# Products with the weights' low parts moved to the end of each step, and the activations' sums begun during the output projection, at an offset of 224 bytes

## The chip, the cores and the metric

The kernel runs on one core of a Trainium2 chip. The metric is device time of one execution in microseconds (us); lower is better. Before the change the median of three runs is 2220.28 us (2219.53 to 2221.06).

The engines are named as in the profile: PE is TensorE, which multiplies (PEld is its loading of the stationary operand); DVE is VectorE; ACT is ScalarE; POOL is GpSimd; SP issues most of the transfers from memory.

## The reference: what is computed

Two layers of a transformer-like trunk on one sequence of 256 tokens, width 2048, in float32:

```python
for l in range(2):
    h = rmsnorm(x, ...)
    x = x + (even_mixer(h, ...) if l == 0 else dilated_attention(h, w_qkv, w_o))
    h = rmsnorm(x, f_norm[l])
    x = x + (silu(h @ w1) * (h @ w3)) @ w2      # 2048 -> 5632 -> 2048
return rmsnorm(x, final_norm)
```

The first layer's mixer has an input projection, an mLSTM and a gated linear recurrence side by side, and an output projection; the second layer's is attention with 16 heads between two projections. Nearly all of the work is products of 256 rows of activations with weights that are read once, about 400 MB in all.

## The kernel before

**Numbers in two parts.** TensorE multiplies float32 at full pace only in a reduced form (fp32r). So each operand is split: a high part, rounded to that form, and a low part, the rest. ScalarE casts the weights to `wh` (line 228) and VectorE subtracts to get `wl` (line 229); activations are stored as pairs in the same way (`xT`, `hT`, `oT`, `ya`, `yb`; index 0 is the high part, 1 the low part). A product is then three products: high by high, high by low, low by high.

**Items and steps.** The weights come in items of 512 contraction rows by 512 columns (1 MB, one transfer into `raw`, three buffers). Each item is two steps, a step being half of its contraction rows. The list `steps` is made beforehand and runs in order; there are 768 steps: 0 to 79 the input projection, 80 to 111 the first output projection, 112 to 375 the first feed-forward network, 376 to 471 the attention's projections, 472 to 503 the second output projection, 504 to 767 the second feed-forward network. `emit_step` (line 340) first calls the step's `before`, if it has one, then issues the splits of the weights up to three steps ahead (`emit_split`; four buffers each for `wh` and `wl`), then the step's matmuls, and then lets every waiting task go on by one piece (`run_tasks`). Every engine carries out its instructions in the order in which they were issued.

**Three forms of a step.**

- Narrow (`narrow`, line 293; matmuls on lines 300 to 302): the activations are stationary, the weights move, 512 columns at a time. For each of 2 blocks of 128 contraction rows and each of 2 halves of the tokens there are three products: `xh` with `hi` (the weights' high part), `xh` with `lo`, `xl` with `hi`. That is 12 matmuls.
- Wide (line 355; matmuls on lines 361 and 362): the weights are stationary. For each of 8 blocks, one matmul of 512 columns (`wh` with the activations' high and low parts side by side) and one of 256 columns (`wl` with the high part): 16 matmuls, 48 such steps in the input projection and 64 in the attention.
- Seven products (`seven_products`, line 304; matmuls on lines 336 to 338): a 2x2 block scheme in the manner of Strassen and Winograd, which needs 7 block products instead of 8, each of three matmuls of 256 columns: 21 matmuls. It is used for `w1`'s items 1 to 3 of every feed-forward chunk but the first, 120 steps in all. It needs sums of weight blocks (`ws`, `wf`, lines 199 to 211, made by VectorE and ScalarE when the item is split) and sums of activation blocks, `sf`.

**The activations' sums.** `act_sums` (line 1056) is a task of each feed-forward network. For the three groups 1, 2 and 3 of the normalized activations it waits until the group is written to `xT` (a flag that the output projection's last work sets), and makes two sums of it, one for each seven-product step: an operation on 512 columns (line 1067), four on 128 columns (1071 to 1075), ScalarE's cast into `sf` (1077), and VectorE's low part (1079). There are five stops (`yield`) for each sum, so five advances of the task, and one advance in each step. The six sums are kept in three slots of 2112 floats, two sums of 1024 floats each in a slot. The task is queued by the `before` of the network's first step, `at_first` (steps 112 and 504):

```python
steps[at_first]["before"] = lambda: queue.append(act_sums())
```

The first chunk of the network has 16 narrow steps. In the second chunk the seven-product steps are the 20th, 21st, 24th, 25th, 28th and 29th after `at_first`, for the contraction blocks 4, 6, 8, 10, 12 and 14. A step that needs a sum that has not been issued lets all tasks go on until it has been (`until`, through `seven`).

**Around the change.** The output projection makes its four column chunks in steps 80 to 111; chunk 2 is steps 96 to 103 and chunk 3 is 104 to 111. When a chunk is done, `norm_evac` adds the residual and writes the chunk's group of `xT` (lines 440 and 441).

**The end.** The last four steps are written out behind the loop: for each half of the tokens, the four steps' products for that half through `narrow`, and then the final norm and the output.

Of the kernel before, what the change touches and what calls it, by code (L numbers as in the profile page):

```python
# [9 lines left out]
F32 = mybir.dt.float32  # L10
F32R = mybir.dt.float32r
# [5 lines left out]
S = 256  # L17
P = 128
# [50 lines left out]
def trunk_kernel(ctx: ExitStack, tc: tile.TileContext, a, out):  # L69
    nc = tc.nc  # L70
    V, A, PE, GP, SP = nc.vector, nc.scalar, nc.tensor, nc.gpsimd, nc.sync
# [12 lines left out]
    mxp = ctx.enter_context(tc.tile_pool(name="mxp", bufs=2, space=PSUM))  # L84
    ctx.enter_context(tc.manual_schedule())

    def slot(shape, dt=F32, name="s8"):
        t = s8p.tile([P, SLOT], dt, tag="s8", name=name)
        n = int(np.prod(shape))
        v = t[:, :n]  # L90
        if len(shape) == 1:
            return v
        pat = {2: "p (a b) -> p a b", 3: "p (a b c) -> p a b c", 4: "p (a b c d) -> p a b c d"}[len(shape)]
        return v.rearrange(pat, **dict(zip("abcd"[1:], shape[1:])))
# [6 lines left out]
    def ev(name="ev"):  # L101
        return evp.tile([P, CW], F32, tag="ev", name=name)
# [4 lines left out]
    def mx(name="mx"):  # L107
        return mxp.tile([P, CW], F32, tag="mx", name=name)
# [44 lines left out]
    steps = []  # L153
# [59 lines left out]
    def emit_split(s):  # L213

        st = steps[s]
        it = st["item"]
        if st["seven"] and st["half"] == 0:
            weight_sums(it)
        raw = loaded[it][:, 2 * st["half"]:2 * st["half"] + 2, :]
        hi = whp.tile([P, 2, CW], F32R, tag="wh", name="wh")  # L220
        lo = wlp.tile([P, 2, CW], F32R, tag="wl", name="wl")
        for k in (0, 1) if s < 2 else (slice(0, 2),):
            if s < 2:
                use_xT(2 * s + k)
            elif s < KB // 2:
                use_xT(2 * s)
                use_xT(2 * s + 1)
            A.copy(hi[:, k], raw[:, k])  # L228
            V.tensor_tensor(lo[:, k], raw[:, k], hi[:, k].bitcast(F32), op=ALU.subtract)  # L229
        splits[s] = (hi, lo)  # L230
        if st["seven"]:
            splits[s] = (hi, lo, [t[:, :, st["half"]] for t in sums[it]])
            if st["last_half"]:
                sums.pop(it)
        if st["last_half"]:
            loaded.pop(it)
            emit_load()
# [31 lines left out]
    urgent, queue, active = [], [], []  # L269
# [8 lines left out]
    def run_tasks():  # L278
        advance(urgent)
        while queue and len(active) < CONC:  # L280
            active.append(queue.pop(0))
        advance(active)
# [8 lines left out]
            assert n < 10000, flag  # L291

    def narrow(st, hi, lo, toks):
        for j in range(2):
            x2 = st["act"](st["kb"] + j)
            f, e = st["first"] and j == 0, st["last"] and j == 1
            for t in toks:
                xh, xl = (x2[:, i, t * P:(t + 1) * P] for i in range(2))
                acc = st["ch"].acc[t]
                PE.matmul(acc, xh, hi[:, j, :], start=f, stop=False)  # L300
                PE.matmul(acc, xh, lo[:, j, :], start=False, stop=False)  # L301
                PE.matmul(acc, xl, hi[:, j, :], start=False, stop=e)  # L302

    def seven_products(st, hi, lo, ts):

        ch = st["ch"]
        a1, a2 = (st["act"](st["kb"] + j) for j in range(2))
        sf = st["seven"](st["kb"])
        if ch.ext is None:
            ch.ext = [accp.tile([P, CW], F32, tag="acc", name="ext") for _ in range(2)]  # L310
            ch.opened = set()
        (c0, c1), (e0, e1) = ch.acc, ch.ext

        def a(x, t):
            return x[:, 0, t * P:(t + 1) * P], x[:, 1, t * P:(t + 1) * P]

        def sa(k):
            return sf[:, k, 0, :], sf[:, k, 1, :]

        def b(j, n):  # L320
            return hi[:, j, n * 256:n * 256 + 256], lo[:, j, n * 256:n * 256 + 256]

        def tb(k):
            return ts[k][:, 0, :], ts[k][:, 1, :]

        todo = [
            (a(a1, 0), b(0, 0), e0, 0), (sa(0), tb(0), e0, 1), (sa(1), tb(1), e1, 0), (sa(2), b(0, 1), e1, 1),
            (a(a2, 0), b(1, 0), c0, 0), (sa(3), b(1, 1), c0, 1), (a(a2, 1), tb(2), c1, 0),
        ]

        for (xh, xl), (wh, wl), dst, n in ([todo[k] for k in (1, 0, 3, 2, 5, 4, 6)] if st["last"] else todo):
            o = dst[:, n * 256:n * 256 + 256]
            new = dst is not c0 and dst is not c1 and id(dst) not in ch.opened
            ch.opened.add(id(dst))
            end = st["last"] and n == 0
            PE.matmul(o, xh, wh, start=new, stop=False)  # L336
            PE.matmul(o, xh, wl, start=False, stop=False)  # L337
            PE.matmul(o, xl, wh, start=False, stop=end)  # L338

    def emit_step(s):  # L340
        st = steps[s]
        if st["before"]:
            st["before"]()
        for f in range(s, min(s + AHEAD + 1, len(steps))):
            if f not in splits and f >= pos["split"]:
                emit_split(f)
                pos["split"] = f + 1
        ch = st["ch"]
        hi, lo, *ts = splits.pop(s)
        if ch.acc is None:  # L350
            if ch.small:
                ch.acc = [mx("acc") for _ in range(2)]
            else:
                ch.acc = [accp.tile([P, CW], F32, tag="acc", name="acc") for _ in range(1 if st["wide"] else 2)]
        if st["wide"]:
            acc = ch.acc[0]
            wh, wl = (w.rearrange("p a (b f) -> p (a b) f", f=P) for w in (hi, lo))
            for j in range(8):
                x2 = st["act"](st["kb"] + j)
                f, e = st["first"] and j == 0, st["last"] and j == 7  # L360
                PE.matmul(acc, wh[:, j, :], x2.rearrange("p a b -> p (a b)"), start=f, stop=False)  # L361
                PE.matmul(acc[:, :S], wl[:, j, :], x2[:, 0, :], start=False, stop=e)  # L362
        elif st["seven"]:
            seven_products(st, hi, lo, *ts)
        else:
            narrow(st, hi, lo, (0, 1))
        run_tasks()
        if st["last"]:
            g = ch.evac(ch)
            if ch.at_once:  # L370
                next(g, None)
            urgent.append(g)
# [87 lines left out]
    def act_norm(gains):  # L460
        def act(kb):
            until(f"xT{gains}_{kb // 4}")
            return act_x(kb)

        return act
# [523 lines left out]
    def ffn(l, gains, nxt):  # L989
        st = {}  # L990
        act = act_norm(gains)
# [62 lines left out]
        sf = {}  # L1054

        def act_sums():

            for g in SEVEN:
                while f"xT{gains}_{g}" not in flags:
                    yield  # L1060
                two = slot((2, 4, 2, P), F32R, "sf")
                for j, kb in enumerate((4 * g, 4 * g + 2)):
                    f = two[:, j]
                    v = ev("sa")
                    x = xT[:, kb:kb + 2].bitcast(F32)
                    vv = v.rearrange("p (j t) -> p j t", j=2)
                    V.tensor_tensor(vv, x[:, :, 0, :], x[:, :, 1, :], op=ALU.add)
                    a11, a21, a12, a22 = (vv[:, j, t * P:(t + 1) * P] for j in range(2) for t in range(2))
                    w = ev("sb").rearrange("p (k t) -> p k t", k=4)
                    yield  # L1070
                    V.tensor_tensor(w[:, 0], a21, a22, op=ALU.add)
                    V.tensor_tensor(w[:, 2], a11, a21, op=ALU.subtract)
                    yield
                    V.tensor_tensor(w[:, 1], w[:, 0], a11, op=ALU.subtract)
                    V.tensor_tensor(w[:, 3], a12, w[:, 1], op=ALU.subtract)
                    yield
                    A.copy(f[:, :, 0, :], w)  # L1077
                    yield
                    V.tensor_tensor(f[:, :, 1, :], w, f[:, :, 0, :].bitcast(F32), op=ALU.subtract)  # L1079
                    sf[kb] = f  # L1080
                    flags.add(f"sf{l}_{kb}")
                    yield
# [5 lines left out]
        at_first = len(steps)  # L1088
        for hidx, (c0, c1) in enumerate(UPS):
# [7 lines left out]
            last = hidx == len(UPS) - 1  # L1097
# [15 lines left out]
            for n, kgs in ((0, range(c0, c1 - 1)), (1, range(c0, c1 - 1)), (0, (c1 - 1,)), (1, (c1 - 1,)),  # L1113
                           (2, range(c0, c1)), (3, range(c0, c1))):
                for kg in kgs:
                    add_unit(a["w2"][l, n][kg], chs[n], 4 * kg, kg == c0, kg == c1 - 1, act_h)
        steps[at_first]["before"] = lambda: queue.append(act_sums())
        return ssq


# [76 lines left out]
    first = len(steps)  # L1197
# [5 lines left out]
    act = act_norm(G_O)  # L1203
# [33 lines left out]
    n = NCD - 1  # L1237
    ch = steps[-1]["ch"]
# [4 lines left out]
    for t in range(2):  # L1243
# [5 lines left out]
        o = ev("out")  # L1249
# [92 lines left out]
```

## Time and profile before

| | us |
|---|---|
| median of three runs | 2220.28 |
| the profiled execution | 2219.59 |
| its span, first to last instruction | 2217.8 |
| matmuls shown, all kinds | 11492 |
| DVE on `wl` (line 229), 770 operations | 928.7 |
| ACT on `wh` (line 228), 770 operations | 794.0 |
| mean granted clock of TensorE | 0.996 |

How to read it: a row of the timeline is start, length, engine, line, operation, the tile written and those read, shape, count, and in brackets the engine's idle time just before with what ended it. Lengths of matmuls overlap, since they are pipelined; what counts is the distance from one start to the next. In a row of the windows there stand the stretch, its length, the busy time of PE, PEld, DVE, ACT and POOL (number of instructions in parentheses), then the granted clock of TensorE as a share of full speed, the share of the DMA engines, and GB/s.

### The profile page before, as it was taken

What the parts mean: (1) busy time and instruction counts of PE and PEld (TensorE: products, weight loads), DVE (VectorE), ACT (ScalarE), POOL (GpSimd) and SP (SyncE); (2) the same over time, 40 slices, a digit from 0 to 9 for tenths busy, and PEclk for the clock granted to TensorE, in tenths of its full rate; (3) what the DMA queues carried; (4) which work ended last, traced back from release to release, by engine and by line L of the source; (5) the groups of instructions that cost most, each with busy time, mean ns of one, the idle gap of its engine ahead of it and who ended that gap; (6) DMA issues with size and microseconds to landing.
All of it is one profiled execution on the core that took longest, in us unless ns stands there. A gap on an engine that the chain in (4) does not pass through costs nothing.

```text
span 2217.8 us, 28894 instructions
## 1 busy us (share of the span) xinstructions
PE 2195.3 (99%) x11492; PEld 1881.5 (85%) x11492; DVE 1588.9 (72%) x2160; ACT 1156.3 (52%) x1555; POOL 22.6 (1%) x37
## 2 busy tenths in 40 slices
PE   9999999999999999999999999999999999999998
PEld 7887888888888888888888888888888888888886
DVE  6877756875787688578666676567867885886686
ACT  6666555544455455445554555455544553554454
POOL 0000000000000000000000000000000000000000
PEclk9999999999999999999999999999999999999999
DMA  7444555555555555555554555455555655555653
GB/s 280 174 143 148 193 201 199 171 190 190 199 181 207 179 201 201 194 197 191 177 191 174 180 185 175 171 182 180 189 190 190 208 190 190 183 203 197 215 192 131
DMA packets 61471, 417.53 MB, mean 188 GB/s; under 512 B 7060, under 2 KB 7956, under 8 KB 12568
## 3 DMA queue, kind: packets, MB, share of 16 engines
q1 hardware_dynamic: 58616, 406.69, 52.9%
q0 software_dynamic: 2288, 8.39, 1.1%
q8 instruction: 90, 1.47, 0.2%
q10 hardware_dynamic: 432, 0.61, 0.1%
q14 instruction: 45, 0.37, 0.0%
HBM read 413.56 MB, written 2.10 MB: 187 GB/s over the span
## 4 chain that ended last, share of the span: by engine, by line
PE 90%; DVE 6%; ACT 2%; issue 1%; DMA 0%; SPq 0%; POOL 0%; POOLq 0%; DVEq 0%; ACTq 0%
PE acc L300 20%; PE acc L301 20%; PE acc L302 20%; PE acc L361 9%; PE acc L362 5%; PE ext L338 2%; PE ext L337 2%; PE ext L336 2%; DVE wl L229 2%; PE acc L338 2%; PE acc L336 2%; PE acc L337 2%; ACT wh L228 1%; PE hTp L146 1%; PE rgp L524 1%
## 5 line engine op out<-in xcount | busy, mean ns | idle before, releaser
L229 DVE TENSOR_TENSOR wl<-raw,wh 128x1024 fp32r<-128x1024 f32 (+1 forms) x770 | 928.7, 1220 | 519.9 <-ACT wh L228 517.1
L228 ACT CAST wh<-raw 128x1024 fp32r<-128x1024 f32 (+1 forms) x770 | 794.0, 1046 | 518.8 <-PE acc L302 376.2
L300 PE MATMUL acc<-wh,xT 128*128 128x512 f32 x1184 | 467.5, 395 | 0.0
L301 PE MATMUL acc<-wl,xT 128*128 128x512 f32 x1184 | 462.9, 391 | 1.0 <-DVE wl L229 1.0
L302 PE MATMUL acc<-wh,xT 128*128 128x512 f32 x1184 | 461.6, 390 | 0.0
L361 PE MATMUL acc<-xT,wh 128*128 128x512 f32 x896 | 321.7, 402 | 0.5 <-ACT v L731 0.5
L300 PE MATMUL acc<-wh,hT 128*128 128x512 f32 x704 | 276.1, 392 | 0.0
L302 PE MATMUL acc<-wh,hT 128*128 128x512 f32 x704 | 274.3, 390 | 0.0
L301 PE MATMUL acc<-wl,hT 128*128 128x512 f32 x704 | 274.1, 389 | 0.1
L302 PEld LDWEIGHTS acc<-wh,xT 128*128 128x128 f32 x1184 | 222.7, 188 | 47.2
L300 PEld LDWEIGHTS acc<-wh,xT 128*128 128x128 f32 x1184 | 223.4, 189 | 45.7 <-issue 1.5
L301 PEld LDWEIGHTS acc<-wl,xT 128*128 128x128 f32 x1184 | 223.1, 188 | 44.9 <-DVE wl L229 2.3
L362 PE MATMUL acc<-xT,wl 128*128 128x256 f32 x896 | 251.2, 280 | 0.2 <-DVE wl L229 0.2
L209 ACT CAST wf<-ws 128x512 fp32r<-128x512 f32 x180 | 111.9, 622 | 201.1 <-DVE ws L202 152.5
L361 PEld LDWEIGHTS acc<-xT,wh 128*128 128x128 f32 x896 | 168.3, 188 | 39.5 <-ACT v L731 0.6
L362 PEld LDWEIGHTS acc<-xT,wl 128*128 128x128 f32 x896 | 169.2, 189 | 1.1 <-DVE wl L229 0.5
L302 PEld LDWEIGHTS acc<-wh,hT 128*128 128x128 f32 x704 | 132.1, 188 | 27.8
L301 PEld LDWEIGHTS acc<-wl,hT 128*128 128x128 f32 x704 | 132.3, 188 | 27.4 <-DVE wl L229 0.5
L300 PEld LDWEIGHTS acc<-wh,hT 128*128 128x128 f32 x704 | 132.2, 188 | 26.8
L210 DVE TENSOR_TENSOR wf<-ws,wf 128x512 fp32r<-128x512 f32 x180 | 113.3, 684 | 0.0
L338 PE MATMUL ext<-wf,sf 128*128 128x256 f32 x240 | 68.7, 286 | 4.6 <-DVE sf L1079 4.6
L336 PE MATMUL ext<-wf,sf 128*128 128x256 f32 x240 | 68.3, 285 | 3.6 <-ACT sf L1077 3.6
(278 smaller groups left out, 2731.8 us busy)
## 6 DMA issues: line engine op xcount, KB each, us to landing
raw<-in_w SPq DMA_DIRECT2D x264, 1024.0 KB, 4.9
raw<-in_w_aqk SPq DMA_DIRECT2D x32, 1024.0 KB, 4.9
raw<-in_w_out SPq DMA_DIRECT2D x16, 1024.0 KB, 4.9
raw<-in_w_av SPq DMA_DIRECT2D x16, 1024.0 KB, 4.9
raw<-in_w_o SPq DMA_DIRECT2D x16, 1024.0 KB, 4.9
raw<-in_w_xr SPq DMA_DIRECT2D x8, 1024.0 KB, 6.8
raw<-in_w_qk SPq DMA_DIRECT2D x8, 1024.0 KB, 4.9
raw<-in_w_og SPq DMA_DIRECT2D x8, 1024.0 KB, 4.8
```

The lines of the kernel that those rows point to most:

```text
L209: A.copy(f[:, 0], t)
L210: V.tensor_tensor(f[:, 1], t, f[:, 0].bitcast(F32), op=ALU.subtract)
L228: A.copy(hi[:, k], raw[:, k])
L229: V.tensor_tensor(lo[:, k], raw[:, k], hi[:, k].bitcast(F32), op=ALU.subtract)
L300: PE.matmul(acc, xh, hi[:, j, :], start=f, stop=False)
L301: PE.matmul(acc, xh, lo[:, j, :], start=False, stop=False)
L302: PE.matmul(acc, xl, hi[:, j, :], start=False, stop=e)
L336: PE.matmul(o, xh, wh, start=new, stop=False)
L337: PE.matmul(o, xh, wl, start=False, stop=False)
L338: PE.matmul(o, xl, wh, start=False, stop=end)
L361: PE.matmul(acc, wh[:, j, :], x2.rearrange("p a b -> p (a b)"), start=f, stop=False)
L362: PE.matmul(acc[:, :S], wl[:, j, :], x2[:, 0, :], start=False, stop=e)
```

## The change

Four edits:

1. `narrow` makes two passes over its blocks and halves: first `xh` with `hi` and `xl` with `hi`, then `xh` with `lo`.
2. `seven_products` makes first the two products with the high parts of all seven, and then the seven products with the low parts, in the order that the last step had before.
3. The wide form makes eight matmuls with `wh`, then eight with `wl`.
4. `act_sums` is queued twelve steps earlier, at `at_first - 12` (steps 100 and 492, in the middle of the output projection's chunk 2), and its tiles begin 56 floats, which is 224 bytes, into their slots.

```diff
-    def slot(shape, dt=F32, name="s8"):
+    def slot(shape, dt=F32, name="s8", off=0):
...
-        v = t[:, :n]
+        v = t[:, off:off + n]
...
     def narrow(st, hi, lo, toks):
-        for j in range(2):
-            x2 = st["act"](st["kb"] + j)
-            f, e = st["first"] and j == 0, st["last"] and j == 1
-            for t in toks:
-                xh, xl = (x2[:, i, t * P:(t + 1) * P] for i in range(2))
-                acc = st["ch"].acc[t]
-                PE.matmul(acc, xh, hi[:, j, :], start=f, stop=False)
-                PE.matmul(acc, xh, lo[:, j, :], start=False, stop=False)
-                PE.matmul(acc, xl, hi[:, j, :], start=False, stop=e)
+        for part in range(2):
+            for j in range(2):
+                x2 = st["act"](st["kb"] + j)
+                for t in toks:
+                    xh, xl = (x2[:, i, t * P:(t + 1) * P] for i in range(2))
+                    acc = st["ch"].acc[t]
+                    if part == 0:
+                        PE.matmul(acc, xh, hi[:, j, :], start=st["first"] and j == 0, stop=False)
+                        PE.matmul(acc, xl, hi[:, j, :], start=False, stop=False)
+                    else:
+                        PE.matmul(acc, xh, lo[:, j, :], start=False, stop=st["last"] and j == 1)
...
-        for (xh, xl), (wh, wl), dst, n in ([todo[k] for k in (1, 0, 3, 2, 5, 4, 6)] if st["last"] else todo):
+        for (xh, xl), (wh, wl), dst, n in todo:
...
             PE.matmul(o, xh, wh, start=new, stop=False)
-            PE.matmul(o, xh, wl, start=False, stop=False)
-            PE.matmul(o, xl, wh, start=False, stop=end)
+            PE.matmul(o, xl, wh, start=False, stop=False)
+        for (xh, xl), (wh, wl), dst, n in (todo[k] for k in (1, 0, 3, 2, 5, 4, 6)):
+            PE.matmul(dst[:, n * 256:n * 256 + 256], xh, wl, start=False, stop=st["last"] and n == 0)
...
-            for j in range(8):
-                x2 = st["act"](st["kb"] + j)
-                f, e = st["first"] and j == 0, st["last"] and j == 7
-                PE.matmul(acc, wh[:, j, :], x2.rearrange("p a b -> p (a b)"), start=f, stop=False)
-                PE.matmul(acc[:, :S], wl[:, j, :], x2[:, 0, :], start=False, stop=e)
+            x2s = [st["act"](st["kb"] + j) for j in range(8)]
+            for j, x2 in enumerate(x2s):
+                PE.matmul(acc, wh[:, j, :], x2.rearrange("p a b -> p (a b)"), start=st["first"] and j == 0, stop=False)
+            for j, x2 in enumerate(x2s):
+                PE.matmul(acc[:, :S], wl[:, j, :], x2[:, 0, :], start=False, stop=st["last"] and j == 7)
...
-                two = slot((2, 4, 2, P), F32R, "sf")
+                two = slot((2, 4, 2, P), F32R, "sf", off=56)
...
-        steps[at_first]["before"] = lambda: queue.append(act_sums())
+        steps[at_first - 12]["before"] = lambda: queue.append(act_sums())
```

More of the change, by code (lines that the diff above doesn't have):

```diff
@@ L334, in seven_products @@
             ch.opened.add(id(dst))
-            end = st["last"] and n == 0
             PE.matmul(o, xh, wh, start=new, stop=False)
-            PE.matmul(o, xh, wl, start=False, stop=False)
-            PE.matmul(o, xl, wh, start=False, stop=end)
+            PE.matmul(o, xl, wh, start=False, stop=False)
+        for (xh, xl), (wh, wl), dst, n in (todo[k] for k in (1, 0, 3, 2, 5, 4, 6)):
+            PE.matmul(dst[:, n * 256:n * 256 + 256], xh, wl, start=False, stop=st["last"] and n == 0)
     def emit_step(s):
```

## The prediction

> **What bounds the kernel now.** I read the page first, its span and its first part, and then the list of what TensorE waited for.
>
> ```profile
> span 2217.8 us, 28894 instructions
> PE 2195.3 (99%) x11492; PEld 1881.5 (85%) x11492; DVE 1588.9 (72%) x2160; ACT 1156.3 (52%) x1555; POOL 22.6 (1%) x37
> ```
> ```profile
> PE ext L338 <- DVE sf L1079: 4.6, 2, 2.3
> PE ext L336 <- ACT sf L1077: 3.6, 2, 1.8
> ...
> PE acc L301 <- DVE wl L229: 1.0, 2, 0.8
> ```
>
> TensorE is busy 2195.3 of 2217.8 us, so it is the bound, and nothing done on VectorE (72%) or ScalarE (52%) counts unless TensorE waits for it. The columns of the waits are total, times and longest. The two largest waits are for `sf`, the activations' sums: 4.6 + 3.6 = 8.2 us, twice each, once per feed-forward layer. Waits for the weights' low part `wl` are small. The change removes no matmul, so it can only win back waits and lost pace. A busy TensorE also hides lost pace, so next I read start times in the timeline around one of the `sf` waits.
>
> ```profile
> 422.42 0.28 PE L336 MATMUL ext<-wh,xT 128*128 128x256 f32 x1
> ...
> 424.94 0.40 PE L300 MATMUL acc<-wh,xT 128*128 128x512 f32 x1
> ...
> 427.68 0.39 PE L300 MATMUL acc<-wh,xT 128*128 128x512 f32 x1
> ...
> 430.40 0.28 PE L336 MATMUL ext<-wh,xT 128*128 128x256 f32 x1
> ...
> 440.90 0.28 PE L336 MATMUL ext<-wh,xT 128*128 128x256 f32 x1
> ...
> 445.57 0.39 PE L336 MATMUL ext<-wf,sf 128*128 128x256 f32 x1 [1.80 <-ACT sf L1077]
> ...
> 448.38 0.58 PE L338 MATMUL ext<-wf,sf 128*128 128x256 f32 x1 [2.31 <-DVE sf L1079]
> 448.76 0.41 PE L336 MATMUL ext<-wh,xT 128*128 128x256 f32 x1
> 448.97 0.41 PE L337 MATMUL ext<-wl,xT 128*128 128x256 f32 x1
> ...
> 458.62 0.39 PE L300 MATMUL acc<-wh,xT 128*128 128x512 f32 x1
> ```
> ```profile
> 440.90:455.90 15.00, 10.88 (x55) 9.65 (x54) 9.36 (x16) 4.77 (x6) 0.00 (x0) 0.77 0.45 147
> ```
>
> A seven-product step runs from 422.42 to 424.94: 2.52 us for 21 matmuls, 0.120 each. The narrow step from 427.68 to 430.40 takes 2.72 us for 12 matmuls, 0.227 each. Four such steps, two seven-product and two narrow, take 430.40 to 440.90 = 10.50 us. The next four, the same work, take 440.90 to 458.62 = 17.72 us, 7.22 us more. Only 1.80 + 2.31 = 4.11 us of that is shown as waiting. The rest is pace: after the waits a 256-column matmul starts every 0.21 us (448.76, 448.97) instead of every 0.120, and the granted clock of that stretch is 0.77 (the column behind POOL in the windows row). The second layer repeats it:
>
> ```profile
> 1550.29 0.28 PE L336 MATMUL ext<-wh,xT 128*128 128x256 f32 x1
> ...
> 1560.79 0.28 PE L336 MATMUL ext<-wh,xT 128*128 128x256 f32 x1
> ...
> 1578.34 0.39 PE L300 MATMUL acc<-wh,xT 128*128 128x512 f32 x1
> ```
>
> 10.50 us, and then 17.55 us: 7.05 us more. Both stalls together cost 7.22 + 7.05 = 14.27 us.
>
> **Part A: the sums begin twelve steps earlier.** The late operand is the last of six sums of a layer, for contraction block 14, used in the second seven-product step after 440.90. The task advances once per step; each sum takes five advances, so six take 30. It is queued at step 112 and its last sum is needed at step 141, 29 steps later: one advance short. What is missing then is issued on the spot, behind VectorE's other work. The rows of the tile `sf` in the first layer, two of VectorE's timeline and two of the windows (the fifth column is VectorE):
>
> ```profile
> L1077 ACT CAST sf<-sb x6: 618/620/622, 374.6 to 444.9; 128x512 fp32r<-128x512 f32 x6
> L1079 DVE TENSOR_TENSOR sf<-sb,sf x6: 680/684/686, 377.9 to 447.6; 128x512 fp32r<-128x512 f32 x6
> ```
> ```profile
> 370.02 0.48 DVE L441 SCALAR_TENSOR_TENSOR xT<-nT,cpk,xT 128x256 fp32r<-128x256 f32 x1 [0.54 <-ACT xT L440]
> ...
> 370.69 0.68 DVE L1067 TENSOR_TENSOR sa<-xT 128x512 f32<-128x512 f32 x1
> ```
> ```profile
> 338.10:370.70 32.60, 32.60 (x153) 27.07 (x152) 18.42 (x25) 17.15 (x27) 0.00 (x0) 1.00 0.54 181
> ...
> 419.80:448.30 28.50, 24.46 (x158) 21.94 (x156) 27.29 (x40) 15.37 (x20) 0.00 (x0) 0.98 0.58 196
> ```
>
> The first sum starts at 370.69 and the last low part ends at 447.6 + 0.68 = 448.3. Twelve narrow steps are 12 x 2.72 = 32.6 us, so it would end near 415.7, against a need at 445.57 - 1.80 = 443.8: 28 us of slack. Its inputs allow this: the last group of `xT` is written at 370.5, and block 12, the first sum that needs it, comes 20 advances after the start, near 338.1 + 20 x 2.72 = 392.5. The cover is VectorE's idle time: in the twelve steps of the projection now used it is busy 18.42 of 32.60 us. About twelve advances, 2.4 sums, land there; from the rows a sum is 0.68 + 0.68 us plus four small operations, which I estimate at 0.3 us each from their size (a quarter of 0.68, and some start-up), so 2.6 us. That is 6.2 us more, 24.6 of 32.6, and TensorE's operands keep their lead. If this cover were gone, the price would be a sum's length, 2.6 us, at the end of the projection. The task issues no DMA and passes nothing on SP's or POOL's queues. What leaves is the crowded stretch, where VectorE works 27.29 of 28.50 us. I take the whole 14.27 us as gain; the bounds are 14.27 and, if some other operand takes the place of one wait, about half, 7.1.
>
> The 224 bytes shift each sum in its slot. No row shows a stationary operand at such an address, so the cost is bounded below by nothing (a gain is excluded, since these products already keep the 0.120 us of all 256-column ones) and above in the first rival. I take nothing: the nearest rows are the sums' own loads at their present address.
>
> **Part B: products with low parts last.** For a narrow step the wait for `wl` moves from the second matmul to the ninth, 7 x 0.227 = 1.59 us later; in a wide step from the second to the ninth too, about 1.8 us. `wh` comes free earlier and `wl` at most one matmul later, which the four buffers absorb. There are three places with a wait to win, with VectorE's and ScalarE's rows beside TensorE's:
>
> ```profile
> 12.35 0.49 PE L300 MATMUL acc<-wh,xT 128*128 128x512 f32 x1
> 13.61 0.50 PE L301 MATMUL acc<-wl,xT 128*128 128x512 f32 x1 [0.76 <-DVE wl L229]
> 13.94 0.39 PE L302 MATMUL acc<-wh,xT 128*128 128x512 f32 x1
> ```
> ```profile
> 11.25 1.05 ACT L228 CAST wh<-raw 128x1024 fp32r<-128x1024 f32 x1 [0.34 <-DMA raw<-in_w_v]
> ```
> ```profile
> 70.25 0.40 PE L361 MATMUL acc<-xT,wh 128*128 128x512 f32 x1
> 70.83 0.38 PE L362 MATMUL acc<-xT,wl 128*128 128x256 f32 x1 [0.18 <-DVE wl L229]
> ```
> ```profile
> 2201.63 0.39 PE L300 MATMUL acc<-wh,hT 128*128 128x512 f32 x1
> 2202.12 0.50 PE L301 MATMUL acc<-wl,hT 128*128 128x512 f32 x1
> 2202.46 0.39 PE L302 MATMUL acc<-wh,hT 128*128 128x512 f32 x1
> ```
>
> At the start, step 2 begins at 12.35 because `wh` is ready at 11.25 + 1.05 = 12.30, behind a DMA; that stays. Its `wl` then costs (13.61 - 12.35 - 0.23) + (13.94 - 13.61 - 0.23) = 1.13 us, which goes, since eight matmuls now cover it. Nothing is saved in steps 0 and 1, which are hidden behind the same 12.30. At 70.25 the gap is 0.58 instead of 0.23, so 0.35 us; at the tail (0.49 - 0.23) + (0.34 - 0.23) = 0.37 us, where four matmuls (0.91 us) now stand ahead of the low parts. Together 1.85 us; bounds zero, if what follows at the start is late by as much, and 2.3.
>
> For narrow and seven-product steps the pace is unchanged: 0.227 and 0.120 hold whichever operand is repeated. In a wide step 512 and 256 columns alternate; now eight of each run in a row. The starts of wide steps, six in the attention and two in the input projection:
>
> ```profile
> 1190.87 0.40 PE L361 MATMUL acc<-xT,wh 128*128 128x512 f32 x1
> ...
> 1207.83 0.40 PE L361 MATMUL acc<-xT,wh 128*128 128x512 f32 x1
> ```
> ```profile
> 263.78 0.39 PE L361 MATMUL acc<-xT,wh 128*128 128x512 f32 x1
> ...
> 269.33 0.39 PE L361 MATMUL acc<-xT,wh 128*128 128x512 f32 x1
> ```
>
> That is 16.96 / 6 = 2.827 us and 5.55 / 2 = 2.775 us a step. The new order should take 8 x 0.227 + 8 x 0.120 = 2.776, plus the cost of going from 256 to 512 columns: the narrow step behind a seven-product one took 424.94 to 427.68 = 2.74, 0.02 more than the next. So 2.796: a gain of 0.03 on each of the 64 steps of the attention, 1.9 us, and -0.02 to 0.03 on the 48 of the input projection, which I take as 0. Bounds: 4 us gained, if all of them reach 2.776, to 1.5 lost, if the change of width costs 0.06 a step in the attention and more in the projection.
>
> **The sum.** 14.3 + 1.85 + 1.9 = 18.0 us. The profiled execution took 2219.59 us, 1.8 more than its span, and lies 0.7 below the median of 2220.28. So 2219.6 - 18.0 = 2201.6 for it, and 2202.3 us for the median.
>
> **The rivals.**
>
> (1) Slower: loads of the shifted sums. Of a seven-product step's 21 matmuls, 12 load a sum as the stationary operand; 120 such steps make 1440.
>
> ```profile
> L336 PEld LDWEIGHTS ext<-wf,sf x240: 186/192/330, 420.2 to 2156.9; 128*128 128x128 f32 x120
> ```
>
> A load takes 0.192 us, yet matmuls follow at 0.120 because loads overlap. If at 224 bytes they could not, each would cost up to 0.072 us: 1440 x 0.072 = 104 us, so 2306. It decides from 18.0 / 1440 = 12.5 ns per product on. Against it: nothing in the profile makes the address matter; for it, only that no row shows such an address. Chance 0.04. [...]
>
> (2) Only part A pays: the start's gain is given back to a late DMA, the wide steps gain nothing or lose 1.5. 2220.3 - 14.3 + (0 to 1.5) = 2206 to 2207.5. For it: the input projection already runs at 2.775. Chance 0.16.
>
> (3) The stall moves: with the sums early, VectorE is still the fullest engine of that stretch, and a weight sum comes late in the first seven-product steps. Half of 14.3 remains: about 2209.5. Against it: later chunks, which have the weight sums but not these, show no such wait among TensorE's. Chance 0.08.
>
> (4) The change does not do what it says: the task starts earlier but stands still until the old place. Then only part B is left: 2220.3 - 3.75 = 2216.5. Chance 0.04.
>
> [...]
>
> **How the numbers follow.** The forecast has 0.68, the rivals 0.04, 0.16, 0.08 and 0.04. The range reaches from part B's best case (2202.3 - 2.6, and 1 us for the run) to rival 2's worst: 2198.7 to 2207.5; (1), (3) and (4), 0.16, lie outside. About 0.2% (4.4 us) is what a measurement of this kernel can tell from no change. Forecast, (2) and (3) are faster, 0.92; (4) is within it, 0.04; (1) slower, 0.04.
>
> **What would show it.** The `sf` rows are gone from TensorE's waits, the last `sf` write of a layer comes near 416 and some 28 us ahead of its first reader, the granted clock stays 1.00 in that stretch, four steps there take 10.5 us, and a wide step of the attention about 2.80. I am wrong if loads of `sf` take over 0.192 us, if TensorE's list shows `wf` or `wh` in that stretch, or if the wide steps take over 2.83.

## The result and the profile after

The changed kernel is faster, by 1.1%: median 2195.01 us (2194.75 to 2196.08, four runs) against 2219.91 us of the kernel before (2218.67 to 2221.06, four runs). The ratio is 0.9889, with a 95% interval of 0.9872 to 0.9906. That is 24.9 us less, where 18.0 were forecast; 2195.01 lies below the range that the prediction gave (2198.7 to 2207.5).

The profiled execution took 2196.08 us, 23.5 less than that of before. The page's span and first part, and the list of what TensorE waited for:

```profile
span 2194.3 us, 29192 instructions
PE 2179.1 (99%) x11492; PEld 1871.9 (85%) x11492; DVE 1591.5 (73%) x2160; ACT 1156.6 (53%) x1555; POOL 21.8 (1%) x37
```
```profile
PE acc L301 <- ACT wh L228: 1.7, 1, 1.7
PE num L798 <- ACT q L765: 1.4, 1, 1.4
PE nT L146 <- DVE xres L416: 1.1, 5, 0.3
PE warm L1129 <- DVE ones L1123: 1.1, 1, 1.1
PE acc L362 <- ACT v L733: 1.0, 1, 1.0
```

The same 11492 matmuls, and all waits for `sf` and `wl` are gone. A wait of 1.7 us for the second half of `wh` in step 0 is new, behind one of the kernel's first transfers. In the new order the fifth matmul needs that half, in the old one the seventh. No kernel with the old order of narrow steps shows this wait; of the 14 other kernels with the new order, 13 show it, between 0.28 and 1.36 us. So the wait comes with the change, and its length scatters. The timeline around the old stall, with the windows row of that stretch (its last columns are granted clock, DMA share, GB/s), the rows of the tile `sf` in the first layer, and the same four steps in the second:

```profile
421.43 0.28 PE L337 MATMUL ext<-wh,xT 128*128 128x256 f32 x1
...
423.88 0.40 PE L301 MATMUL acc<-wh,xT 128*128 128x512 f32 x1
...
426.63 0.39 PE L301 MATMUL acc<-wh,xT 128*128 128x512 f32 x1
...
429.35 0.28 PE L337 MATMUL ext<-wh,xT 128*128 128x256 f32 x1
...
439.75 0.28 PE L337 MATMUL ext<-wh,xT 128*128 128x256 f32 x1
...
450.14 0.39 PE L301 MATMUL acc<-wh,xT 128*128 128x512 f32 x1
```
```profile
439.75:454.75 15.00, 15.00 (x88) 13.26 (x87) 10.42 (x14) 6.20 (x8) 0.00 (x0) 1.00 0.59 206
```
```profile
L1079 ACT CAST sf<-sb x6: 618/620/623, 337.5 to 407.4; 128x512 fp32r<-128x512 f32 x6
L1081 DVE TENSOR_TENSOR sf<-sb,sf x6: 684/686/687, 342.7 to 415.6; 128x512 fp32r<-128x512 f32 x6
```
```profile
1547.57 0.28 PE L337 MATMUL ext<-wh,xT 128*128 128x256 f32 x1
...
1557.96 0.39 PE L301 MATMUL acc<-wh,xT 128*128 128x512 f32 x1
```

The four steps that took 17.72 us take 450.14 - 439.75 = 10.39 us, at a granted clock of 1.00; in the second layer, where they took 17.55, they also take 10.39. The last sum ends at 415.6 + 0.7 = 416.3. So far this is the forecast. But 10.39 is less than the 10.50 of undisturbed steps before: the seven-product step from 421.43 to 423.88 takes 2.45 us, not 2.52, while the narrow step from 426.63 to 429.35 still takes 2.72. Over all 120 seven-product steps the median from start to start falls from 2.520 to 2.463 us. That is the part that was not forecast.

Where the 23.5 us came from, by the starts of the steps in the two profiled executions:

| stage | forecast | measured |
|---|---|---|
| input projection (steps 0 to 79) | -1.5 | -1.0 |
| the two stalls for the sums | -14.3 | -14.3 |
| attention (steps 376 to 471) | -1.9 | -1.9 |
| last four steps | -0.4 | -0.4 |
| seven-product steps, pace | 0 | -6.0 |

The stalls' row is -7.33 and -7.16 us for steps 140 to 143 and 532 to 535, less 0.23 for the faster pace of the four seven-product steps in them; the last row is 2.90 and 2.89 us for the rest of the two feed-forward networks, and those 0.23.

The wide steps of the attention took the time that the prediction gave them. These are the starts of two consecutive ones, and of the fifth after the first:

```profile
1179.21 2.00 PE L362 MATMUL acc<-xT,wh 128*128 128x512 f32 x8
1182.00 2.00 PE L362 MATMUL acc<-xT,wh 128*128 128x512 f32 x8
...
1193.18 2.00 PE L362 MATMUL acc<-xT,wh 128*128 128x512 f32 x8
```

Five steps in 13.97 us are 2.794 us each; 2.796 was forecast and 2.827 measured before.

### The profile page after: what moved, and what is told of

Same layout as the page of the kernel before. It is cut to its first block, busy times and chain, and to the rows that moved or that the text cites. A ratio compares the mean times of both kernels' runs of the same rounds, so it can differ in the third digit from the quotient of the medians.

```text
span 2194.3 us, 29192 instructions
## 1 busy us (share of the span) xinstructions
PE 2179.1 (99%) x11492; PEld 1871.9 (85%) x11492; DVE 1591.5 (73%) x2160; ACT 1156.6 (53%) x1555; POOL 21.8 (1%) x37
## 4 chain that ended last, share of the span: by engine, by line
PE 95%; DVE 2%; ACT 1%; DMA 1%; issue 1%; POOL 0%; SPq 0%; POOLq 0%; DVEq 0%; ACTq 0%
PE acc L301 21%; PE acc L302 21%; PE acc L304 21%; PE acc L362 9%; PE acc L364 5%; PE ext L337 3%; PE ext L340 3%; PE ext L338 3%; PE acc L338 2%; PE acc L340 2%; PE acc L337 2%; PE hTp L146 1%; DMA raw<-in_w_v 1%; DVE wl L229 1%; PE rgp L526 1%
## 5 line engine op out<-in xcount | busy, mean ns | idle before, releaser
L304 PE MATMUL acc<-wl,xT 128*128 128x512 f32 x1184 | 316.8, 389 | 0.0
L362 PE MATMUL acc<-xT,wh 128*128 128x512 f32 x896 | 228.8, 397 | 1.0 <-ACT v L733 1.0
L304 PE MATMUL acc<-wl,hT 128*128 128x512 f32 x704 | 189.0, 389 | 0.0
L362 PEld LDWEIGHTS acc<-xT,wh 128*128 128x128 f32 x896 | 162.4, 189 | 31.1 <-ACT v L733 1.1
L364 PEld LDWEIGHTS acc<-xT,wl 128*128 128x128 f32 x896 | 122.2, 190 | 8.9
L364 PE MATMUL acc<-xT,wl 128*128 128x256 f32 x896 | 124.9, 282 | 0.0
L340 PE MATMUL ext<-wf,sf 128*128 128x256 f32 x240 | 66.9, 279 | 0.0
L337 PE MATMUL ext<-wf,sf 128*128 128x256 f32 x240 | 61.5, 280 | 0.0
```

Of the source, the lines that this page charges most:

```text
L304: PE.matmul(acc, xh, lo[:, j, :], start=False, stop=st["last"] and j == 1)
L340: PE.matmul(dst[:, n * 256:n * 256 + 256], xh, wl, start=False, stop=st["last"] and n == 0)
```

## The experiments

There are two theories for the pace of the seven-product steps: it comes from the address of the sums, or from the new order of the products. Four kernels tell them apart, and separate the parts of the change.

**No offset.** The changed kernel with

```diff
-                two = slot((2, 4, 2, P), F32R, "sf", off=56)
+                two = slot((2, 4, 2, P), F32R, "sf")
```

> The changed kernel with the activations' sums at the start of their slots again (offset 0); all else as changed. A seven-product step took 2.52 us before (0.120 us a matmul) and 2.46 us in the changed kernel. If the address of the sums makes that difference, the steps return to 2.52 us and the time rises by 120 x 0.055 = 6.6 us, to about 2202 us. If the new order of the seven products makes it, the steps stay at 2.46 us and the time at about 2195 us. If it takes both, 2.52 us and 2202 us as with the address.

2201.98 us, ratio to the kernel before 0.9920 (0.9903 to 0.9936). Below stand one seven-product step, the loads of the sums in all such steps, and then the same loads in the changed kernel (minimum, median and maximum in ns):

```profile
420.47 0.28 PE L337 MATMUL ext<-wh,xT 128*128 128x256 f32 x1
...
422.99 0.40 PE L301 MATMUL acc<-wh,xT 128*128 128x512 f32 x1
```
```profile
L337 PEld LDWEIGHTS ext<-wf,sf x240: 187/192/192, 418.1 to 2138.5; 128*128 128x128 f32 x120
```
```profile
L337 PEld LDWEIGHTS ext<-wf,sf x240: 187/188/189, 419.1 to 2133.3; 128*128 128x128 f32 x120
```

The step takes 2.52 us, as with the old order, so the new order alone doesn't make the pace; the address is needed. The loads of the sums change with it: 192 ns with the sums at a multiple of 256 bytes, 188 at 224. And without the offset the kernel stands at 2201.98 us, against the forecast of 2202.3.

**Offset only.** The kernel before with `off` added to `slot` and `off=56` for the sums.

> The kernel before with one edit: the sums 224 bytes into their slots. The sums still start late and all orders are the old ones. If the address alone makes the faster pace, seven-product steps take 2.46 us instead of 2.52 us and the time falls by 6.6 us, to about 2213 us, with the two stalls for the sums (14.3 us) still there. If the order makes it, or it takes both, 2.52 us and about 2220 us.

2213.53 us, ratio 0.9972 (0.9960 to 0.9984).

```profile
422.80 0.28 PE L336 MATMUL ext<-wh,xT 128*128 128x256 f32 x1
...
425.27 0.40 PE L300 MATMUL acc<-wh,xT 128*128 128x512 f32 x1
```

The step takes 2.47 us with the old order, and the stalls are still there: 6.4 us come from one number in an address.

**Old order inside a seven-product step.** The changed kernel with the loop over the seven products as it was before.

> The changed kernel with the old order inside a seven-product step (high by high, high by low, low by high for each product in turn); early sums, the 224 bytes and the other new orders stay. If the address alone makes the faster pace: steps of 2.46 us and about 2195 us. If the order alone, or both together: steps of 2.52 us and about 2202 us.

2195.85 us, ratio 0.9890 (0.9876 to 0.9905); the median step takes 2.471 us, against 2.463, and the step that was quoted for the changed kernel runs here so:

```profile
421.01 0.28 PE L338 MATMUL ext<-wh,xT 128*128 128x256 f32 x1
...
423.48 0.40 PE L301 MATMUL acc<-wh,xT 128*128 128x512 f32 x1
```

The order of the products in this form is worth about 0.008 us a step, 1 us in all. The theory of the order falls.

**Early sums only.** The kernel before with

```diff
-        steps[at_first]["before"] = lambda: queue.append(act_sums())
+        steps[at_first - 12]["before"] = lambda: queue.append(act_sums())
```

> The kernel before with one edit: the sums' task is queued twelve steps earlier. No offset, old orders. All theories: the two stalls go, four steps behind 440 us take 10.5 us instead of 17.7, and the time falls by 14.3 us to about 2205.6 us; seven-product steps stay at 2.52 us, wide steps of the attention at 2.83 us. The rival to this, that half of the stall moves to another operand, gives about 2212.5 us.

2206.30 us, ratio 0.9938 (0.9923 to 0.9953), 13.6 us less.

```profile
441.32 0.28 PE L336 MATMUL ext<-wh,xT 128*128 128x256 f32 x1
...
451.82 0.39 PE L300 MATMUL acc<-wh,xT 128*128 128x512 f32 x1
```

The four steps take 10.50 us, as long as undisturbed ones, so nothing of the stall moved to another operand (the prediction's rival 3). The three parts now stand one by one: early sums 13.6 us, the new orders 2206.30 - 2201.98 = 4.3 us, the offset 2201.98 - 2195.01 = 7.0 us (6.4 by itself). 13.6 + 4.3 + 7.0 = 24.9.

**Other offsets.** What is it about the address? All slots of the program begin at multiples of 256 bytes, and so do `xT` and the tiles of `wh`, `wl` and `wf`. The changed kernel with another number in `off`, one run each:

> The changed kernel with the sums 32 bytes into their slots instead of 224. Theory line: what helps is that a sum's 512 bytes do not start on a 256-byte boundary, any distance from one will do; then a seven-product step takes about 2.46 us as at 224. Theory distance: the gain grows with the distance from the boundary, so at 32 bytes little of it is left, 2.51 us. (At 0 bytes it is 2.52 us.)

> The changed kernel with the sums 128 bytes into their slots. Theory line: 2.46 us a seven-product step. Theory distance: the middle of a 256-byte line is as far as one can get from a boundary, so as good as 224 bytes or better, 2.46 us or less. If only odd multiples of 32 bytes help, 2.52 us.

> The changed kernel with the sums 256 bytes into their slots. Theory line and theory distance: a boundary again, so 2.52 us a step and about 2202 us. Theory order of places: what helps is merely that the sums lie elsewhere relative to the other operands, as any shift does; then 2.46 us and about 2195 us.

> The changed kernel with the sums 192 bytes in. Steps took 2.520 us at 0, 2.487 at 32, 2.499 at 128, 2.461 at 224 and 2.520 at 256 bytes. If odd multiples of 32 bytes are better than even ones, 192 gives about 2.50 us; if it is nearness to the next boundary, 2.46 to 2.48 us.

> The changed kernel with the sums 240 bytes in, an odd multiple of 16. If odd multiples of 32 bytes are what helps, about 2.50 us or worse; if it is nearness to the next boundary, 2.46 us or less, and with it a time of 2195 us or a little below.

> The changed kernel with the sums 208 bytes in. Steps took 2.476 us at 192, 2.463 at 224 and 2.495 at 240 bytes. If the pace follows the address smoothly, about 2.47 us; if the values jump about with every place, anything from 2.45 to 2.51 us. A step under 2.46 us would make this the fastest version.

| bytes into the slot | median step, us | time, us |
|---|---|---|
| 0 | 2.520 | 2201.98 (four runs) |
| 32 | 2.486 | 2198.46 |
| 128 | 2.499 | 2197.95 |
| 192 | 2.476 | 2196.40 |
| 208 | 2.471 | 2195.47 |
| 224 | 2.463 | 2195.01 (four runs) |
| 240 | 2.495 | 2197.93 |
| 256 | 2.520 | 2204.87 |

256 bytes are as good as none, so it isn't a matter of mere distance from where the slot began. Each of the six places between helps, by 0.02 to 0.06 us a step. Neither distance from the boundary, nor odd or even multiples of 32 bytes, nor nearness to the next boundary puts the rest in order. Of the eight, 224 has the shortest step. (Single times carry the start's scatter: the kernel at 256 bytes reached step 80 at 273.56 us, that at 0 bytes at 270.13.)

**The weights' sums shifted instead, and both.** Tiles of 1088 floats for `wf`, begun at 224 bytes, with nine small-tile buffers for ten:

```diff
-EV_BUFS = 10
+EV_BUFS = 9
...
-            f = m4((4, 256), "wf", F32R).rearrange("p (i a) b -> p i a b", i=2)
+            f = m4((4, 256), "wf", F32R, off=56).rearrange("p (i a) b -> p i a b", i=2)
```

> The changed kernel with the sums at offset 0 and, in their place, the weights' sums wf 224 bytes into their tiles (wider tiles, and one buffer of ten taken from the pool of small tiles to make room). wf is the moving operand of 9 of the 21 matmuls of a seven-product step; the sums are the stationary operand of 12. If what counts is how the two operands lie to each other, a shift of the moving one helps as well: steps between 2.46 and 2.52 us. If what counts is the stationary operand's own address, 2.52 us as with no shift. If every read across a boundary costs, more than 2.52 us.

> Both the sums and the weights' sums 224 bytes in. If how the operands lie to each other counts, 6 of the 12 matmuls with a sum (those with wf) lose their gain, and the steps lie between 2.46 and 2.52 us, about 2.49. If the stationary operand's own address counts, 2.46 us.

One run each gave 2197.79 and 2197.34 us, with median steps of 2.493 and 2.478 us. Shifting the moving operand helps as well, though the sums stand at multiples of 256 bytes then; and the loads of the sums for products with `wf` fall to 188 ns, without any shift of their own:

```profile
L337 PEld LDWEIGHTS ext<-wf,sf x240: 187/188/193, 418.5 to 2134.9; 128*128 128x128 f32 x120
```

Shifting both is worse than the sums alone. That speaks for the place of the two operands relative to each other. In both kernels the operands of 9 of the 21 products stand at different places, yet the steps differ by 0.015 us, so the number of such products doesn't set the size by itself.

**The same shift on 512-column products.** The changed kernel with `off=56` on `hT`, the stationary operand of the narrow steps of `w2`.

> The changed kernel with the feed-forward networks' second activations (hT) also 224 bytes into their slots; they are the stationary operand of 2112 narrow matmuls with 512 columns, one every 0.2267 us. If the address acts on every load of a stationary operand in the same way as with the sums (0.120 to about 0.117 us a matmul over 21 of which 12 load a sum), narrow matmuls on hT come down to 0.222 to 0.224 us, and the time by 6 to 10 us, to 2185 to 2189 us. If it acts only where a load is longer than the matmul it hides behind (0.19 us against 0.12), they stay at 0.2267 us and the time at 2195 us.

Both theories of the expectation missed: 2208.53 us, 13.5 us slower than the change. Two narrow steps of that stretch:

```profile
2013.93 0.39 PE L301 MATMUL acc<-wh,hT 128*128 128x512 f32 x1
...
2019.53 0.39 PE L301 MATMUL acc<-wh,hT 128*128 128x512 f32 x1
```

They take 2.80 us a step, 0.233 a matmul, instead of 2.72 and 0.227. What helps 256-column products harms 512-column ones. 176 such steps at 0.08 us are 14 us, the whole loss.

**Own address or relation.** Wider tiles for `wh` and `wl`, begun at 224 bytes (and nine small-tile buffers); then the same with `hT` at 224 bytes.

```diff
-        hi = whp.tile([P, 2, CW], F32R, tag="wh", name="wh")
-        lo = wlp.tile([P, 2, CW], F32R, tag="wl", name="wl")
+        hi = whp.tile([P, 1088], F32R, tag="wh", name="wh")[:, 56:1080].rearrange("p (a b) -> p a b", a=2)
+        lo = wlp.tile([P, 1088], F32R, tag="wl", name="wl")[:, 56:1080].rearrange("p (a b) -> p a b", a=2)
```

> The changed kernel with the moving operands wh and wl 224 bytes into wider tiles (one small-tile buffer of ten given up for room); xT, hT and the other stationary operands stay on multiples of 256 bytes, the sums at 224. A narrow step on hT took 2.72 us with both on multiples of 256 bytes and 2.80 us with hT alone at 224. If it matters how the two operands lie to each other, narrow steps now take about 2.80 us too, and some 530 of them add up to about 40 us: 2235 us. If it is the stationary operand's own address, they stay at 2.72 us and the time at about 2195 us.

> The same, and hT at 224 bytes too, so that on hT both operands lie off the multiples by the same distance. If it matters how they lie to each other: narrow steps on hT are back at 2.72 us, those on xT slow as in the run before. If the stationary operand's own address matters: 2.80 us on hT, 2.72 us on xT, about 2209 us in all.

One run each gave 2232.80 and 2220.25 us. Two narrow steps of `w2` in the first kernel, then two in the second, and one of the second on `xT`:

```profile
2036.59 0.40 PE L301 MATMUL acc<-wh,hT 128*128 128x512 f32 x1
...
2042.19 0.40 PE L301 MATMUL acc<-wh,hT 128*128 128x512 f32 x1
```
```profile
2026.71 0.39 PE L301 MATMUL acc<-wh,hT 128*128 128x512 f32 x1
...
2032.15 0.39 PE L301 MATMUL acc<-wh,hT 128*128 128x512 f32 x1
```
```profile
431.06 0.40 PE L301 MATMUL acc<-wh,xT 128*128 128x512 f32 x1
433.86 0.28 PE L337 MATMUL ext<-wh,xT 128*128 128x256 f32 x1
```

With the weights alone shifted: 2.80 us. With `hT` shifted by as much: 5.44 / 2 = 2.72 us again, while `xT`, still at a multiple of 256 bytes, stays at 2.80. So on narrow steps it isn't the stationary operand's own address that counts but whether both operands lie at the same place within 256 bytes.

The first of the two kernels also shows the two widths apart. In a wide step `wh` and `wl` are the stationary operands and `xT` moves, eight products of 512 columns and then eight of 256; two of its wide steps in the attention begin like this:

```profile
1197.71 2.03 PE L362 MATMUL acc<-xT,wh 128*128 128x512 f32 x8
1199.58 1.09 PE L364 MATMUL acc<-xT,wl 128*128 128x256 f32 x8
1200.52 2.03 PE L362 MATMUL acc<-xT,wh 128*128 128x512 f32 x8
```
```profile
1179.21 2.00 PE L362 MATMUL acc<-xT,wh 128*128 128x512 f32 x8
1181.05 1.12 PE L364 MATMUL acc<-xT,wl 128*128 128x256 f32 x8
1182.00 2.00 PE L362 MATMUL acc<-xT,wh 128*128 128x512 f32 x8
```

The second group is the changed kernel's. With the weights shifted, the eight products of 512 columns take 1.87 us instead of 1.84, and the eight of 256 columns 0.94 instead of 0.95. Over all 64 such steps the medians between the starts of the first and the last of the 256-column products are 0.818 and 0.832 us, 0.117 and 0.119 a matmul. The same shift slows one width and speeds the other.

**A small shift of `hT`.** `off=8` in place of 56.

> The changed kernel with hT 32 bytes into its slots. With the sums, 32 bytes gave somewhat over half of what 224 gave (2.487 against 2.463 us, from 2.520). If the loss on hT follows the same course, narrow steps on hT take about 2.76 us and the time is about 2202 us; if any shift costs the same, 2.80 us and 2209 us; if only 224 is bad, 2.72 us and 2195 us.

One run gave 2208.09 us, and 2.80 us a narrow step: 32 bytes cost as much as 224. In the shifts tried, 512-column products know only two paces: one for the same place, one for different places.

## Why the prediction was right, and where it was wrong

**Part A was right.** The stalls were worth 14.3 us in the profiles, as read from the steps' starts, and 13.6 us by the experiment with early sums only. The sums ended at 416.3 us, forecast near 415.7. The waits alone, 8.2 us, would have been too little. Behind the waits of 1.80 and 2.31 us the granted clock was 0.50 before the change:

```profile
448.40:452.00 3.60, 3.60 (x17) 3.60 (x18) 0.00 (x0) 0.00 (x0) 0.00 (x0) 0.50 0.46 193
```

That belongs to the price, and it went with the waits: in the changed kernel's windows row the granted clock is 1.00.

**Part B was right in sum.** Forecast 3.75 us, measured 4.3 between the two kernels that differ by it. The attention gave 1.9, the tail 0.4. At the start step 2 gave 1.17 us of the 1.13 forecast; step 20 gave 0.74 instead of 0.35, since the prediction counted one late matmul of that step and not what followed it; step 1 gave 0.24; but in the profiled execution 0.8 us was lost in step 0 to the wait named above, and 0.5 in step 12, which waited 0.97 us for `v` instead of 0.47. Its bound of 4 us for the wide steps doesn't follow from its rows: 64 x (2.827 - 2.776) = 3.3 us, with which the range would begin at 2199.4.

**The step that failed** is the one on the 224 bytes: "a gain is excluded, since these products already keep the 0.120 us of all 256-column ones", and "I take nothing: the nearest rows are the sums' own loads at their present address". The pace of 0.120 us was common to all 256-column products while all their operands stood at the same place within 256 bytes; it wasn't a floor. In a run of 21 it falls to 2.463 / 21 = 0.117 us. Over 1440 matmuls with a sum as stationary operand the gain is 6.4 to 7.0 us, 4.4 to 4.9 ns each, or 2.7 ns over all 2520 of the seven-product steps. With that term at nothing the forecast, 2202.3 us, is the time of the kernel without the offset, 2201.98 us. That these agree to 0.3 us is partly luck: part A gave 0.7 less than forecast, part B 0.5 more.

There was a warning for this in the profile of before. Loads of the sums took 0.192 us, and loads in narrow steps 0.188 (the mean of 1184 on line 302); wide steps of the same work took 2.775 us in one place and 2.827 in another. A pace that differs between places with the same work need not be a floor. The prediction also argued the address from one side only: rival 1 gave the shift a price and no prize. The runs show both: with the sums, steps of 2.463 us at 224 bytes and 2.495 at 240, against 2.520 at 0; with `hT` a loss at 224 bytes, 2.80 us a narrow step against 2.72.

**Shown and not shown.** That the relation of the two operands' addresses within 256 bytes sets the pace of narrow steps is shown by the pair of runs with `wh`, `wl` and `hT`. That 256-column products gain by a shift which makes 512-column ones lose is shown by the wide steps with `wh` and `wl` shifted. For seven-product steps the run with `wf` shifted alone fits the same cause, but its operands are mixed; no run shifts both operands of all 256-column products alike, and the size by offset follows no order that these runs reveal. Why 512-column products lose by a difference of places and 256-column ones gain stays open. A shift of the stationary operands of all narrow steps wasn't tried, since `hT` showed a loss at both distances. No version tried is faster than the changed kernel.

## What to carry to other kernels

A stall's price is read from the starts of equal work before and behind it, not from the waits: here 4.1 us of waits cost 7.2 us in one layer and 7.05 in the other. When every matmul keeps the same odd pace, look at where the operands stand in memory before you call it a floor; a shift of a few dozen bytes costs one number to try, and its sign has to be measured for each form of product. And when an edit carries a number without a visible reason, bound its effect on both sides: that no row shows an effect is no reason to put it at nothing.

## What the runs showed of the hardware

Two things were unexpected. In these runs a 256-column matmul with its own load follows the one before at 0.120 us when stationary and moving operands stand at the same place within 256 bytes (2.520 / 21 in the kernel without the offset; 0.832 / 7 = 0.119 in the changed kernel's wide steps), and at about 0.117 on average when the stationary ones of 12 in 21 are shifted by 224 (2.463 / 21), or when those of a wide step are (0.818 / 7). In narrow steps a 512-column one keeps 0.227 us (2.72 / 12) when they stand at the same place, and takes 0.233 (2.80 / 12) when they don't: with `hT` moved by 32 or by 224 bytes, and with `wh` and `wl` moved by 224. Loads and matmuls overlap in these runs, since a load of a sum takes 0.188 us and the matmuls of its step follow at 0.117. Still, moving either operand's address changes the pace, by up to 3% (2.72 to 2.80 us a narrow step).

The kernel before also has products in plain float32. Two of them, 256 columns each, shown as four records, and what follows:

```profile
109.03 1.02 PE L751 MATMUL qkp<-qkT 128*128 128x256 f32 x4
109.99 0.73 PE L754 MATMUL nMb<-nMs,ehr 4*128 4x512 f32 x2
```

They take 0.96 us, 0.48 each, where a 256-column product of the reduced form takes 0.120.
